# A full 128-row tile for the low part of the keys in a split-precision attention

## The chip, the cores and the metric

The program runs on one NeuronCore of one Trainium2 chip. Its time is device microseconds (us) from the first to the last of its work, as the median of three runs. One more execution was recorded by the hardware profiler; all rows below come from that one. TensorE (PE in the rows; PEld is its loading of stationary operands) multiplies, VectorE (DVE) and ScalarE (ACT) do the elementwise work, GpSimd (POOL) does a part of it, and SyncE (SP) issues the transfers.

## The reference, cut to what matters

One layer of a diffusion backbone on 1024 latent tokens (a grid of 16 rows by 64 columns) and 128 context tokens, width 1024, 8 heads of 64. Queries and keys come from one projection; a latent query attends in one softmax to a window of keys around it and to 128 cached context keys; a context query attends to the 128 context tokens:

```python
s_band = jnp.einsum('bhqd,bhikd->bhqik', q_r, k_b).astype(jnp.float32) * SCALE
s_band = s_band + bias[None].astype(jnp.float32)
s_band = jnp.where(col_mask[None, None, :, None, :], s_band, -jnp.inf)
s_ctx = jnp.einsum('bhqd,bhld->bhql', q_r, k_ctx).astype(jnp.float32) * SCALE
s = jnp.concatenate([s_band.reshape(b, h, GRID_W, n_band), s_ctx], axis=-1)
p = jax.nn.softmax(s, axis=-1).astype(v.dtype)
```

Beside the attention there are a gated short convolution, projections of both, two normalisations and a feed-forward part of width 4096. All of it is float32.

## The kernel before, in words

**Split precision.** A float32 operand is held as two parts: a high part rounded to float32r (a cast) and a low part (the value minus the high part). A product is the sum of high by high, high by low and low by high, each a TensorE matmul into the same accumulator.

**Stages.** First the modulation and the values V (to some 85 us of the span). Then the queries and keys of head 0 as dense products (lines 364, 366 and 368, the three matmuls of a contraction block). Then the attention proper: 8 heads of 9 units each, 72 units. Units 0 to 7 of a head are (column block, row half): 128 latent queries against 384 window keys and the 128 cached keys. Unit 8 holds the 128 context queries against 128 context keys. After the attention come gates and projections, the output projection, and the feed-forward part.

**One unit.** `scores(n)` issues the matmuls of the scores; VectorE adds bias and mask and takes the row extremum (line 561), ScalarE takes the exponential (563), VectorE the reciprocal and the scaling (566, 567). One unit later `transposes(n)` turns the probabilities by TensorE (576), and ScalarE and VectorE split them (210, 211). Two units later, for each pair of units, `pv` multiplies them with the values (600 to 610, and 593 and 594 for the context). Between these, TensorE gets dense matmuls: 72 for each head, the projection of the next head's queries and keys, dealt out by the table SHARES; for the last head it is a gate product. All orders are written out by hand; each engine runs its own list in that order, and waits by semaphores.

**The operands of a score.** A head has 64 dimensions, half of the 128 rows of TensorE's array. Tile `qs` holds the high part of the queries on 64 rows and their low part on the other 64; which half is which depends on the parity of the head (`ev` is the half of the high part). Tile `kh` holds the high part of the keys twice, on both halves, so that one matmul over 128 rows gives high by high and low by high together (lines 554, 555, and 549 for the context). Tile `kl` holds the low part of the keys on the rows `ev` alone, and a head of the other parity uses the other half of the same tile. Its matmuls (556, 557, and 550 for the context) therefore take 64 rows of `qs` and 64 rows of `kl`. The four matmuls of a unit are 384, 128, 384 and 128 columns wide and go to one bank. `kl` is written by VectorE (line 439, out of a dense product) and GpSimd (line 436, the cached keys).

Of the kernel before, what the change touches and what calls it, by code (L numbers as in the profile page):

```python
# [12 lines left out]
F32 = mybir.dt.float32  # L13
F32R = mybir.dt.float32r
# [4 lines left out]
P = 128  # L19
D = 1024  # L20
KB = D // P
NLAT = 1024
NCTX = 128
# [14 lines left out]

WCOL = (0, 8, 24, 32)
MOFF = (16, 8, 8, 0)  # L40
# Dense products issued with each unit of a head's attention, which spread them evenly over its length.
SHARES = (8, 8, 9, 7, 9, 7, 9, 7, 8)
CTYPE = (0, 1, 1, 2)
# Per chunk of tokens: (row half, first row in the half, offset in the chunk, rows; no rows: the context).
QPIECES = (((0, 0, 0, 6),), ((0, 6, 0, 2), (1, 0, 128, 4)), ((1, 4, 0, 4), (0, 0, 256, 0)))


def tail_len(c):
    """Blocks of the second feed-forward product that a chunk of tokens ends with, token tile by token tile."""
    return 5 if c == NCH - 1 else 2  # L50


def window_masks():
    """Additive masks of the clamped window: [row half a][column kind][query (8 x 16)][key (12 x 32)]."""
    out = np.zeros((2, 3, P, 12 * 32), np.float32)
    for a in range(2):
        for kind, c in enumerate((0, 1, 3)):
            for r in range(8):
                qr = 8 * a + r
                sr = min(max(qr - WR // 2, 0), ROWS - WR)  # L60
                kr = 4 * a + np.arange(12)
                okr = (kr >= sr) & (kr < sr + WR)
                for q in range(16):
                    qc = 16 * c + q
                    sc = min(max(qc - WC // 2, 0), GW - WC)
                    kc = WCOL[c] + np.arange(32)
                    okc = (kc >= sc) & (kc < sc + WC)
                    out[a, kind, r * 16 + q] = np.where(okr[:, None] & okc[None, :], 0.0, NEG).reshape(-1)
    return out


class Ring:
    """Weight blocks [128, <=1024]: loaded in the order of their use, split into two float32r parts."""

    def __init__(self, nc, pool, name, seq, raw_bufs, bufs):
        self.nc, self.pool, self.name, self.seq = nc, pool, name, seq
# [4 lines left out]
        self.more = None  # L81

    def extend(self, pool):
        """From here on one more buffer of each kind, in a pool of its own."""
        self.more = pool, self.nload, self.nhi

    def tile(self, dtype, tag, i, bufs, kind):
# [61 lines left out]
def emit(nc, tc, ctx, aps, outs):  # L149
# [60 lines left out]
        nc.scalar.copy(hi, src)  # L210
        vec.tensor_tensor(out=lo, in0=src, in1=f32(hi), op=ALU.subtract)  # L211

    # ---------------------------------------------------------------- constants
    ident = const.tile([P, P], F32, name="ident")
    ones = const.tile([P, 2], F32, name="ones")
    vec.memset(ones, 1.0)
# [14 lines left out]

    h = [act_chunk() for _ in range(NCH)]

    # ---------------------------------------------------------------- modulation of the mixers' input, V
    with ExitStack() as s0:
        p0 = pool_on(s0, "p0", side="right")
        act(sil, cs, AF.Sigmoid)
# [116 lines left out]
                v_mm(b, t, kb, kb == 0, kb == KB - 1)  # L354
            v_out(b, t)

    # ---------------------------------------------------------------- dense products, channel-major
    def chunk_mm(b, w, c, kbs=KB, woff=0, src=None, first=True, last=True):
        hi, lo = w
        a = src or h[c]  # L360
# [11 lines left out]
        for _ in g:  # L372
            pass

    # ---------------------------------------------------------------- attention
    with ExitStack() as s2:
        p2 = pool_on(s2, "p2", side="right")
        mask = p2.tile([P, 6, 384], BF16, name="mask")
        kl = p2.tile([P, NTOK + NCTX], F32R, name="kl")
        bms = [p2.tile([P, 512], F32, name=f"bm{i}") for i in range(2)]  # L380
        for b_ in bms:
            pl.memset(b_, 0.0)
# [8 lines left out]
        jobs = []  # L391

        def flush_act():
            """Issue ScalarE's parts of the waiting small jobs; returns VectorE's."""
            todo, jobs[:] = jobs[:], []
            for fa_, _ in todo:
                fa_()
            return [fd for _, fd in todo]
# [5 lines left out]
        def dense_qk(hh):  # L404
            ck = cks.pop(hh)
            w = ring.take(ahead=0)
            qs = p2.tile([P, NTOK], F32R, tag="qs", name=f"qs{hh}", bufs=2)
            kh = p2.tile([P, NTOK + NCTX], F32R, tag="kh", name=f"kh{hh}", bufs=2)
            ev = slice(0, 64) if hh % 2 == 0 else slice(64, 128)
            od = slice(64, 128) if hh % 2 == 0 else slice(0, 64)  # L410
            qk[hh] = (qs, kh, ev)
            def pieces(c, b):
                for a, r0, o, nr in QPIECES[c]:
                    if nr:
                        src = b[0:64, o:o + nr * GW].rearrange("p (r c q) -> p r c q", c=4, q=16)
                        yield (src,) + tuple(x[:, :NLAT].rearrange("p (a c r q) -> p a r c q", a=2, c=4, r=8)
                                             [:, a, r0:r0 + nr] for x in (qs[ev], qs[od], f32(qs)[ev]))
                    else:
                        yield b[0:64, o:o + NCTX], qs[ev, NLAT:], qs[od, NLAT:], f32(qs)[ev, NLAT:]

            def qk_act(c, b):
                sl = slice(c * CH, (c + 1) * CH)
                if c == 1:
                    nc.scalar.copy(kh[:, NTOK:], ck)
                nc.scalar.copy(kh[64:128, sl], b[64:128, :CH])
                for src, dh, _, _ in pieces(c, b):
                    nc.scalar.copy(dh, src)
                if c == NCH - 1:
                    kf = p2.tile([P, NCTX], F32, tag="kf", name=f"kf{hh}", bufs=1)
                    nc.scalar.copy(kf[64:128], b[64:128, CH - NCTX:CH])  # L430
                    dma(outs["nk"][hh], kf[64:128])

            def qk_vec(c, b):
                sl = slice(c * CH, (c + 1) * CH)
                if c == 1:
                    pl.tensor_tensor(out=kl[ev, NTOK:], in0=ck[ev], in1=f32(kh)[ev, NTOK:], op=ALU.subtract)
                for src, _, dl, dhf in pieces(c, b):
                    vec.tensor_tensor(out=dl, in0=src, in1=dhf, op=ALU.subtract)
                vec.tensor_tensor(out=kl[ev, sl], in0=b[64:128, :CH], in1=f32(kh)[64:128, sl], op=ALU.subtract)
                (pl if hh else vec).tensor_copy(kh[0:64, sl], f32(kh)[64:128, sl])  # L440

            for c in range(NCH):
                b = next_dense()
                yield from chunk_mm(b, w, c)
                jobs.append((lambda c=c, b=b: qk_act(c, b), lambda c=c, b=b: qk_vec(c, b)))
# [93 lines left out]

        def scores(n):  # L540
            hh, c, a = units[n]
            qs, kh, ev = qk[hh]
            sb = bank(3 + n % 2)
            s = p2.tile([P, 512], F32, tag="s", name=f"s{n}", bufs=2)
            st = p2.tile([P, 4], F32, tag="st", name=f"st{n}", bufs=4)
            qa = q_ap(qs, c, a)
            qh = q_ap(qs[ev], c, a)
            if c == 4:
                mm(sb[:, :P], lhsT=qa, rhs=kh[:, NLAT:NTOK], start=True, stop=False)
                mm(sb[:, :P], lhsT=qh, rhs=kl[ev, NLAT:NTOK], start=False, stop=True)  # L550
                w = P
                bm = bms[0][:, 384:512]
            else:
                mm(sb[:, :384], lhsT=qa, rhs=k_ap(kh, c, a), start=True, stop=False)
                mm(sb[:, 384:], lhsT=qa, rhs=kh[:, NTOK:], start=False, stop=False)
                mm(sb[:, :384], lhsT=qh, rhs=k_ap(kl[ev], c, a), start=False, stop=False)  # L556
                mm(sb[:, 384:], lhsT=qh, rhs=kl[ev, NTOK:], start=False, stop=True)
                w = 512
                bm = bms[n % 2]
            dve = flush_act()  # L560
# [129 lines left out]
        run(filler)  # L690
        flush_all()

    # ---------------------------------------------------------------- mixers' projections
    mB = pool_on(ctx, "mB", bufs=4)
    acp = pool_on(s3, "acp", side="right", bufs=8)
    tp = pool_on(s3, "tp", side="right", bufs=2)
# [15 lines left out]
                later.popleft()()  # L712

    def gemv_rest():
        """The modulation after the mixers: g1, sh2, sc2, g2 of both conditionings, 512 columns at a time."""
        ones_r = gp.tile([P, 2], F32R, name="ones_r")
        nc.scalar.copy(ones_r, ones)
        for g in range(8):
# [200 lines left out]
            split(mc[0][:, j], mc[1][:, j], mix[j][:, csl(c)])  # L919
    s3.close()  # L920

    # ---------------------------------------------------------------- output projection, first norm
    x9 = pool_on(ctx, "x9")
    wx = pool_on(ctx, "wx")
    ring.extend(wx)
# [19 lines left out]
    HALVES = (slice(0, 512), slice(512, 1024))  # L945

    def norm(t, gr, br, out, done=None, adder=vec, parts=(slice(0, D),)):
        """Closures that normalise t (in place) and write t * g + b to out."""
        m = tmp(fp, [P, 4], "bag", 6)

        def stats():
# [21 lines left out]
        return [stats, scale, apply, last]  # L973

    def weave(lists):
        """The closures of three tiles in an order in which no engine waits long for another."""
        a, b, c = lists
        return [a[0], a[1], b[0], a[2], b[1], c[0], b[2], c[1], a[3], c[2], b[3], lambda: None, c[3]]

# [36 lines left out]
        return go  # L1016

    def token_mm(banks, a, i, w, first, last, kb=None):
        """banks[half] += a[token tile i]^T @ w, a = (hi, lo) parts [128, (kb,) tokens]."""
        ts_ = slice(i * P, (i + 1) * P)  # L1020
        ah, al = (a[0][:, kb, ts_], a[1][:, kb, ts_]) if kb is not None else (a[0][:, ts_], a[1][:, ts_])
        for half in range(2):
# [27 lines left out]
        bg.extend(weave(parts))  # L1050
        later.extend(make_h2(c, kb) for kb in range(KB))

    # ---------------------------------------------------------------- feed-forward, second norm
    s6 = ExitStack()
    rows2 = {}

# [6 lines left out]
        rows2["ln2b"] = row(r2, "ln2b", aps["ln2b"])  # L1063

    def residual(t):
        """x1 becomes ALPHA * x1 + b2 * g2, all of the second sum but the product."""
        def go():
            if t == 8:
                r = tmp(fp, [P, D], "lnt", 3)
# [39 lines left out]
        return [first] + q[1:]  # L1109

    def ln2_final(t, ps):
        """The last token tile: each half of its columns as soon as its products are done."""
        r = tmp(fp, [P, D], "lnt", 3)
        m = tmp(fp, [P, 4], "bag", 6)
        s_ = tmp(fp, [P, 2, 6], "bst", 2)
# [148 lines left out]
```

## Time and profile before

| what | value |
|---|---|
| median of three runs | 1708.21 us (1706.99 to 1708.92) |
| span of the profiled execution | 1707.4 us |
| TensorE busy with matmuls | 1674.1 us, 98% of the span |
| VectorE, ScalarE, GpSimd busy | 965.0, 666.8, 219.2 us |
| heaviest lines | 364, 366, 368: 1632 matmuls each, some 552 us each |
| mean traffic to and from memory | 115 GB/s |

The page gives the span of the profiled execution and no other time of it. The median of the runs is 0.8 us above that span, and this is what lies around it. A busy share is an average over the stages; the rows below come mostly from the attention, between 97 and 328 us.

### The profile page before, as it was taken

To read this page: it belongs to the slowest core of one execution; us is meant where nothing else is said; L and a number is where in the kernel's file an instruction comes from. 1 tells how busy PE (TensorE), PEld (TensorE's weight loads), DVE (VectorE), ACT (ScalarE), POOL (GpSimd) and SP (SyncE) were. 2 spreads that over 40 slices of the span, in tenths; PEclk is the share of its full clock that TensorE was granted. 3 is DMA by queue.
4 is the path that set the end of the run, shared out by engine and by line. 5 is a ranking of instruction groups with operands and counts; after the bars stand their busy time and mean duration, and the time that the engine had idled before them with its cause. 6 is when DMAs were issued, how large, how long until landed. Compare 5 with 4: busy or idle time off the path is not lost.

```text
span 1707.4 us, 23233 instructions
## 1 busy us (share of the span) xinstructions
PE 1674.1 (98%) x8984; PEld 1534.1 (90%) x8984; DVE 965.0 (57%) x1504; ACT 666.8 (39%) x1132; POOL 219.2 (13%) x218
## 2 busy tenths in 40 slices
PE   7999999999999999999999999999999999999997
PEld 5799999999999999998779999998999998999996
DVE  6567778654555565245786556546644445644446
ACT  5366767611122121133454453333433333433332
POOL 2145555200000002110220000000100000100002
PEclk9999999999999999999999999999999999999998
DMA  8332121123222222116433345333443333444332
GB/s 315 132 90 68 46 68 47 45 95 104 83 91 81 87 81 93 51 38 225 145 123 124 123 138 171 130 131 110 166 142 124 124 123 124 136 163 131 126 123 74
DMA packets 86327, 196.01 MB, mean 115 GB/s; under 512 B 32305, under 2 KB 33969, under 8 KB 86217
## 3 DMA queue, kind: packets, MB, share of 16 engines
q1 hardware_dynamic: 86072, 194.52, 34.4%
q8 instruction: 70, 1.15, 0.3%
q14 instruction: 41, 0.33, 0.1%
q10 hardware_dynamic: 144, 0.01, 0.0%
HBM read 186.86 MB, written 7.63 MB: 114 GB/s over the span
## 4 chain that ended last, share of the span: by engine, by line
PE 92%; DVE 5%; DMA 1%; ACT 1%; issue 1%; ACTq 0%; DVEq 0%; SPq 0%
PE ps L368 17%; PE ps L364 17%; PE ps L366 17%; PE ps L1024 8%; PE ps L1023 8%; PE ps L1026 8%; PE ps L800 2%; PE ps L801 2%; PE ps L802 2%; PE ps L576 2%; PE ps L556 1%; DVE wl L126 1%; PE ps L301 1%; DMA wr<-wo 1%; PE ps L303 1%; PE ps L260 1%
## 5 line engine op out<-in xcount | busy, mean ns | idle before, releaser
L364 PE MATMUL ps<-ahi,wh 128*128 128x384 f32 x1632 | 552.1, 338 | 0.0
L368 PE MATMUL ps<-ahi,wl 128*128 128x384 f32 x1632 | 551.9, 338 | 0.0
L366 PE MATMUL ps<-alo,wh 128*128 128x384 f32 x1632 | 551.2, 338 | 0.0
L126 DVE TENSOR_TENSOR wl<-wr,wh 128x1024 fp32r<-128x1024 f32 (+1 forms) x258 | 321.6, 1271 | 120.3 <-ACT wh L113 120.1
L364 PEld LDWEIGHTS ps<-ahi,wh 128*128 128x128 f32 x1632 | 306.5, 188 | 8.6 <-issue 1.4
L366 PEld LDWEIGHTS ps<-alo,wh 128*128 128x128 f32 x1632 | 306.5, 188 | 7.1
L368 PEld LDWEIGHTS ps<-ahi,wl 128*128 128x128 f32 x1632 | 306.4, 188 | 3.2
L113 ACT CAST wh<-wr 128x1024 fp32r<-128x1024 f32 (+1 forms) x266 | 262.6, 1022 | 41.4 <-DMA wr<-wo 18.4
L1023 PE MATMUL ps<-wh,fh 128*128 128x512 f32 x550 | 215.3, 391 | 1.3 <-ACT fh L210 1.3
L1024 PE MATMUL ps<-wl,fh 128*128 128x512 f32 x550 | 216.1, 393 | 0.0
L1086 ACT ACTIVATE rt<-ps,b1c 128x384 f32<-128x384 f32 x96 | 55.9, 582 | 402.5 <-PE ps L368 402.5
L1087 DVE TENSOR_TENSOR rt<-rt 128x384 f32<-128x384 f32 x96 | 53.6, 558 | 273.0 <-ACT rt L1086 273.0
L1026 PE MATMUL ps<-wh,fl 128*128 128x512 f32 x550 | 170.5, 391 | 0.0
L1026 PEld LDWEIGHTS ps<-wh,fl 128*128 128x128 f32 x550 | 103.3, 188 | 21.9
L1023 PEld LDWEIGHTS ps<-wh,fh 128*128 128x128 f32 x550 | 103.2, 188 | 21.7 <-ACT fh L210 2.1
L1024 PEld LDWEIGHTS ps<-wl,fh 128*128 128x128 f32 x550 | 103.3, 188 | 18.9
L965 POOL TENSOR_TENSOR lnt<-lnt,ln2g 128x1024 f32<-128x1024 f32 x8 | 19.2, 2397 | 718.7 <-ACT lnt L964 704.5
L741 DVE SCALAR_TENSOR_TENSOR acc<-wmb,sil,acc 128x512 f32<-128x512 f32 x112 | 81.6, 773 | 27.5 <-DMA wmb<-wmb 27.5
L211 DVE TENSOR_TENSOR fl<-rt,fh 128x384 fp32r<-128x384 f32 x92 | 51.4, 559 | 53.3 <-ACT fh L210 53.3
L210 ACT CAST fh<-rt 128x384 fp32r<-128x384 f32 x92 | 47.2, 513 | 57.9 <-DVE rt L1087 57.9
L563 ACT ACTIVATE s<-s,st 128x512 f32<-128x512 f32 (+1 forms) x72 | 49.6, 688 | 51.3 <-DVE st L561 51.3
L800 PE MATMUL ps<-ach,wh 128*128 128x384 f32 x192 | 65.1, 339 | 0.0
(217 smaller groups left out, 2094.4 us busy)
## 6 DMA issues: line engine op xcount, KB each, us to landing
wr<-w SPq DMA_DIRECT2D x192, 512.0 KB
wmb<-wmb SPq DMA_DIRECT2D x64, 256.0 KB
wr<-wo SPq DMA_DIRECT2D x24, 512.0 KB
mr<-wma SPq DMA_DIRECT2D x16, 512.0 KB
xt<-xt SPq DMA_DIRECT2D x8, 576.0 KB
xk<-xk SPq DMA_DIRECT2D x9, 512.0 KB
vraw<-vd SPq DMA_DIRECT2D x136, 32.0 KB
wr<-wqk SPq DMA_DIRECT2D x8, 512.0 KB
```

Source lines behind the costliest of these rows:

```text
L113: self.nc.scalar.copy(hi[:, :w], self.raw[i][:, :w])
L126: engine.tensor_tensor(out=lo[:, :w], in0=self.raw.pop(i)[:, :w], in1=hi.bitcast(F32)[:, :w], op=ALU.subtract)
L364: mm(b[:, :CH], lhsT=hi[:, ws], rhs=a[0][:, kb, :], start=first and kb == 0, stop=False)
L366: mm(b[:, :CH], lhsT=hi[:, ws], rhs=a[1][:, kb, :], start=False, stop=False)
L368: mm(b[:, :CH], lhsT=lo[:, ws], rhs=a[0][:, kb, :], start=False, stop=last and kb == n - 1)
L741: vec.scalar_tensor_tensor(out=a, in0=t, scalar=sil[:, k, cond:cond + 1], in1=a, op0=ALU.mult, op1=ALU.add)
L800: mm(b[:, :CH], lhsT=hi[:, ws], rhs=parts[kb][0][:, cs_], start=kb == 0, stop=False)
L1023: mm(banks[half], lhsT=ah, rhs=w[0][:, HALVES[half]], start=first, stop=False)
L1024: mm(banks[half], lhsT=ah, rhs=w[1][:, HALVES[half]], start=False, stop=False)
L1026: mm(banks[half], lhsT=al, rhs=w[0][:, HALVES[half]], start=False, stop=last)
L1086: act(rt, b[:, :CH], AF.Relu, bias=b1c[:, f:f + 1])
L1087: vec.tensor_tensor(out=rt, in0=rt, in1=rt, op=ALU.mult)
```

## The change

The one tile `kl` becomes two, `kls[0]` and `kls[1]`, one for each parity of the head. The half that a parity does not use is set to zero once by GpSimd before the attention. The matmuls on the low part of the keys take all 128 rows of `qs` and of the tile; the low part of the queries then meets zeros. The writers of `kl` write the same rows as before, in the tile of their head. The second tile takes 5120 more bytes of each partition, which moves the tiles that are allocated behind it. Comments were removed too, and the lines behind this place have numbers higher by three or four.

```diff
-        kl = p2.tile([P, NTOK + NCTX], F32R, name="kl")
+        kls = [p2.tile([P, NTOK + NCTX], F32R, name=f"kl{i}") for i in range(2)]
+        for i in range(2):
+            pl.memset(kls[i][64 - 64 * i:128 - 64 * i].bitcast(F32), 0.0)
...
-            qk[hh] = (qs, kh, ev)
+            kl = kls[hh % 2]
+            qk[hh] = (qs, kh, kl)
...
             qa = q_ap(qs, c, a)
-            qh = q_ap(qs[ev], c, a)
             if c == 4:
                 mm(sb[:, :P], lhsT=qa, rhs=kh[:, NLAT:NTOK], start=True, stop=False)
-                mm(sb[:, :P], lhsT=qh, rhs=kl[ev, NLAT:NTOK], start=False, stop=True)
+                mm(sb[:, :P], lhsT=qa, rhs=kl[:, NLAT:NTOK], start=False, stop=True)
...
-                mm(sb[:, :384], lhsT=qh, rhs=k_ap(kl[ev], c, a), start=False, stop=False)
-                mm(sb[:, 384:], lhsT=qh, rhs=kl[ev, NTOK:], start=False, stop=True)
+                mm(sb[:, :384], lhsT=qa, rhs=k_ap(kl, c, a), start=False, stop=False)
+                mm(sb[:, 384:], lhsT=qa, rhs=kl[:, NTOK:], start=False, stop=True)
```

On GpSimd, at the head of the attention, this stands in its list before (bm are the bias tiles, kl the low keys, kh the high keys, ck the cached keys, E the bias table; what an instruction waits for is in brackets):

```order
L382 MEMSET bm_790 128x512 [waits PE_49]
L382 MEMSET bm_791 128x512 [waits DMAHW2_49,DMAHW1_49,DVE_49]
L529 TENSOR_TENSOR bm_790<-E_801,mask 128x384 [waits DMAHW1_49,Activation_49,Pool_49]
L436 TENSOR_TENSOR kl<-ck_799,kh_824 64x128 [waits DMAHW7_49,PE_49,Activation_49]
L529 TENSOR_TENSOR bm_791<-E_801,mask 128x384 [waits Pool_49]
```

and this after the change:

```order
L382 MEMSET kl_789 64x1280 [waits Pool_49]
L382 MEMSET kl_790 64x1280 [waits PE_49]
L385 MEMSET bm_793 128x512 [waits Pool_49]
L385 MEMSET bm_794 128x512 [waits DMAHW2_49,DMAHW1_49,DVE_49]
L533 TENSOR_TENSOR bm_793<-E_804,mask 128x384 [waits DMAHW1_49,Activation_49,Pool_49]
L440 TENSOR_TENSOR kl_789<-ck_802,kh_827 64x128 [waits DMAHW7_49,Activation_49]
L533 TENSOR_TENSOR bm_794<-E_804,mask 128x384 [waits Pool_49]
```

Two instructions are added ahead of the others; the wait for PE that the first bias tile had stands at the second of them. On TensorE the order is the same instruction for instruction. At the first unit of the first head it reads before (qs the queries, ps the accumulator):

```order
L554 MATMUL ps_932<-kh_824,qs_823 128x384 [waits DVE_49,Activation_49]
L555 MATMUL ps_932<-kh_824,qs_823 128x128
L556 MATMUL ps_932<-kl,qs_823 128x384
L557 MATMUL ps_932<-kl,qs_823 128x128 [waits Pool_49]
L364 MATMUL ps_961<-ahi_94,wh_857 128x384 [waits PE_49]
```

and after the change:

```order
L557 MATMUL ps_935<-kh_827,qs_826 128x384 [waits DVE_49,Activation_49]
L558 MATMUL ps_935<-kh_827,qs_826 128x128
L559 MATMUL ps_935<-kl_789,qs_826 128x384 [waits Pool_49]
L560 MATMUL ps_935<-kl_789,qs_826 128x128 [waits Pool_49]
L364 MATMUL ps_964<-ahi_94,wh_860 128x384 [waits PE_49]
```

The third matmul has got a wait for GpSimd, once in the program. On VectorE, ScalarE and SyncE the lists and what their instructions wait for read the same.

## Rows read from the trace of the kernel before

**Rows 1.** Windows: busy us (x instructions) per engine; then clock, DMA share, GB/s

```profile
97.50:328.00 230.50, 228.94 (x1449) 207.11 (x1447) 179.42 (x459) 158.11 (x395) 118.91 (x146) 1.00 0.20 54
375.00:450.00 75.00, 75.00 (x429) 74.12 (x429) 37.70 (x58) 13.38 (x23) 0.00 (x0) 1.00 0.27 92
```

**Rows 2.** Waits of TensorE, 97.5 to 328: total us, times, longest

```profile
PE ps L554 <- DVE kh L440: 0.8, 1, 0.8
PE ps L593 <- DVE attnT L621: 0.8, 1, 0.8
```

**Rows 3.** Timeline of TensorE's matmuls around one unit: start, duration, engine, line, tiles, shapes

```profile
125.63 0.34 PE L554 MATMUL ps<-kh,qs 128*128 128x384 f32 x1
125.81 0.22 PE L555 MATMUL ps<-kh,qs 128*128 128x128 f32 x1
125.96 0.44 PE L556 MATMUL ps<-kl,qs 64*128 64x384 f32 x1
126.24 0.22 PE L557 MATMUL ps<-kl,qs 64*128 64x128 f32 x1
126.39 0.45 PE L364 MATMUL ps<-ahi,wh 128*128 128x384 f32 x1
126.67 0.34 PE L366 MATMUL ps<-alo,wh 128*128 128x384 f32 x1
```

**Rows 4.** Timeline of TensorE's weight loads around the same unit

```profile
125.63 0.19 PEld L555 LDWEIGHTS ps<-kh,qs 128*128 128x128 f32 x1
125.96 0.18 PEld L556 LDWEIGHTS ps<-kl,qs 64*128 64x128 f32 x1
...
126.39 0.19 PEld L364 LDWEIGHTS ps<-ahi,wh 128*128 128x128 f32 x1
```

**Rows 5.** Groups by shape, TensorE, 97.5 to 325: busy us, mean ns | idle

```profile
L556 PE MATMUL ps<-kl,qs 64*128 64x384 f32 x64 | 28.3, 442 | 0.0
```

**Rows 6.** Timeline of TensorE in the modulation: a matmul over 4 rows

```profile
54.82 0.60 PE L268 MATMUL ps<-sel,rows 4*128 4x2 f32 x4
55.35 0.50 PE L301 MATMUL ps<-wh,ahi 128*128 128x512 f32 x1
55.69 0.39 PE L302 MATMUL ps<-wl,ahi 128*128 128x512 f32 x1
```

**Rows 7.** Timeline of TensorE: one 128-column transpose between dense matmuls

```profile
127.03 0.35 PE L364 MATMUL ps<-ahi,wh 128*128 128x384 f32 x1
127.21 0.27 PE L576 MATMUL ps<-ident,s 128*128 128x128 f32 x1
...
127.49 0.33 PE L368 MATMUL ps<-ahi,wl 128*128 128x384 f32 x1
```

**Rows 8.** Timeline of TensorE: a context unit

```profile
123.22 0.28 PE L549 MATMUL ps<-kh,qs 128*128 128x128 f32 x1
123.42 0.32 PE L550 MATMUL ps<-kl,qs 64*128 64x128 f32 x1
...
123.96 0.34 PE L368 MATMUL ps<-ahi,wl 128*128 128x384 f32 x1
```

**Rows 9.** Timeline of VectorE in the seventh and eighth unit of a head

```profile
205.25 1.08 DVE L567 TENSOR_SCALAR s<-s,st 128x512 f32<-128x512 f32 x1
...
206.85 0.68 DVE L561 CUSTOM_DVE_ANT_0 s<-ps,bm 128x512 f32<-128x512 f32 x1
...
208.98 0.49 DVE L567 TENSOR_SCALAR s<-s,st 128x512 f32<-128x512 f32 x1
```

**Rows 10.** Timeline of TensorE: the transposes of these two units

```profile
206.96 0.60 PE L576 MATMUL ps<-ident,s 128*128 128x128 f32 x4
...
210.28 0.60 PE L576 MATMUL ps<-ident,s 128*128 128x128 f32 x4
```

**Rows 11.** Timeline of GpSimd at the head of the attention

```profile
80.90 0.99 POOL L382 MEMSET bm<- 128x512 f32 x2 [24.82 <-PE ps L302]
94.00 0.92 POOL L529 TENSOR_TENSOR bm<-E,mask 128x384 f32<-128x384 f32 x1 [12.11 <-DMA vraw<-vd]
```

More of the change, by code (lines that the diff above doesn't have):

```diff
@@ L541, in scores @@
             hh, c, a = units[n]
-            qs, kh, ev = qk[hh]
+            qs, kh, kl = qk[hh]
             sb = bank(3 + n % 2)
```

## The prediction

> **What bounds the kernel now.** I first cut the span into stages by busy time, since the change touches only the attention. From 97.5 to 328 us TensorE is busy 228.94 of 230.50 us, VectorE 179.42, ScalarE 158.11 and GpSimd 118.91 [rows 1]: TensorE is the limit, the next engine has a fifth of the stage free, and TensorE's granted clock is 1.00, its 2.4 GHz level, throughout. Busy time alone doesn't prove it, because a matmul that waits for its weights counts as busy; so I read the waits next. In the whole stage TensorE waits for others only twice, 0.8 us each [rows 2]. A microsecond taken from TensorE's own list in this stage therefore comes off the end, as long as the others keep up. What a matmul should cost is read in a stretch of dense matmuls, nearly all of 384 columns: 429 in 75.00 us, so 0.175 us each [rows 1], whose weights are all there in time.
>
> Then I read the timeline of one unit by starts, not by durations (durations overlap) [rows 3]. L554 to L555 takes 0.18, as it should. L555, 128 columns, to L556 takes 0.15. L556, 384 columns, to L557 takes 0.28 in place of 0.175. L557 to the dense L364 takes 0.15, and L364 to L366 again 0.28. The loads say why: the load for L555 starts with the matmul before it (125.63, the start of L554), but the load for L556 starts only at 125.96, with its own matmul, and so does that for L364 at 126.39 [rows 4, 3]. These are the two places where a 128-row operand is followed by a 64-row one or the other way about. It is so in every unit: L556 has a mean of 442 ns over all 64 [rows 5], against 0.34 us for L554 of the same width [rows 3]. It isn't the bank or the strided keys: the dense L364 behind the unit, another bank and plain operands, lasts 0.45 us as well [rows 3], and in the modulation a matmul over 4 rows is followed by a 512-column one of 0.50 us, where the next has 0.39 [rows 6].
>
> **The change part by part.** *The score matmuls.* All four take 128 rows, so both places go. What the same four matmuls then cost has to be taken from full-row neighbours. A 384-column one is 0.175. A 128-column one between wider ones is shown by the single transpose: from the dense matmul ahead of it to the second behind it 127.49 - 127.03 = 0.46 us, less two of 0.175, is 0.11 [rows 7]; it doesn't reach 0.175/3 = 0.058, since the next load takes longer than 128 columns. The zeros stream like any other rows: L554, full, and L556, half, differ only by the exposed load. From the start of L555 to the second dense matmul before: 126.67 - 125.81 = 0.86 [rows 3]. After: 0.11 + 0.175 + 0.11 + 0.175 = 0.57. That is 0.29 us for each of 64 units, 18.6 us.
>
> *The context units.* From L549 to the second dense matmul 123.96 - 123.22 = 0.74 [rows 8]. After: 0.11 + 0.11 + 0.175, and 0.06 by which the record of L549 (0.28, against 0.22 for L555) stands ahead of its weights: 0.455. That is 0.285 for each of 8, 2.3 us. Together 20.9 us.
>
> The ends of this term: below, nothing, if the row count isn't the cause; above, a 128-column matmul at its bare 0.058, another 0.104 in each unit, 28 us in all. I take 0.11, which full-row rows of this stage show; the transpose differs from a score matmul only in its operand.
>
> *What could take it back.* Between the end of the scores and the transposes of the same unit lie the leaving of this unit's 64-row tile (0.15 + 0.28 against 0.11 + 0.175, so 0.145) and the next unit's four matmuls (0.29): VectorE and ScalarE lose some 0.43 us of time to finish. The tightest place that repeats is the seventh unit of a head, where VectorE's L567 takes 1.08 us: it ends at 206.33 and its transposes start at 206.96 [rows 9, 10], so 0.63 are free now and 0.2 will be. In the eighth unit VectorE is already late (its L561 at 206.85 starts as soon as it is done with the unit before): L567 ends at 209.47, the transposes start at 210.28 [rows 9, 10], 0.81 free, from which 0.43 goes and another 0.29 because VectorE doesn't move while TensorE does: about 0.1 is left. So the cover just holds. The first of the two waits of rows 2, in the second unit of all, gets longer, since its releaser runs in VectorE's pace; 0.1 to 0.3 us. I put 0.4 us on all of this.
>
> *The added memsets.* Two of 64x1280 on GpSimd. Two of 128x512 took 0.99 us [rows 11]; by columns two of 1280 take 2.5, at the least (by elements) 1.2. GpSimd sits idle for 12.11 us before its first bias tile at 94.00 [rows 11], so they cost nothing; without that cover 2.5 us once. The new wait of the first L556 for GpSimd comes at 98, long after. The queues of SyncE, VectorE and ScalarE stay as they are, and so does every stage behind the attention, which starts earlier and is otherwise the same.
>
> Sum: 20.9 - 0.4 = 20.5 us off a span of 1707.4, so 1686.9; with the 0.8 us that the median stands above it, 1687.7 us.
>
> **A rule that speaks against it.** In the rows, loads are hidden within one row count: in the dense stretches each load starts with the matmul before it (the full-row load for L555 at 125.63 under the full-row L554) [rows 3, 4]. The Trainium skill ("TensorE: Matmul & The Clock Gate", "The mechanism" in Part 3) says the reverse, that a weight load overlaps a running matmul only when the two use different row groups. By it the full-row loads of L556, L557 and L364 would all be exposed. The trace contradicts it, by 429 matmuls at 0.175 us.
>
> **The rivals.** *The loads of four matmuls on one set of rows stay exposed.* Then the two costs stay, and L557, hidden now by its 64-row neighbour, pays the 0.105 of an exposed load too (0.28 - 0.175): 72 times 0.105 is 7.6 us more, 1715.8. It decides if the load for the third score matmul starts with its own matmul. Against it stand the dense rows; for it only that no row shows one stationary operand loaded four times in a row (twice, for L554 and L555, it is hidden). It is the case by the rule above. Chance 0.03.
>
> *VectorE takes the place of the limit.* If its lateness adds up from the seventh unit to the first of the next head, and the margins of 0.1 and 0.2 us are overdrawn, TensorE waits at some four units of each head by up to 0.3 us each: 8 x 4 x 0.3 = 9.6 back, 1697. For it: 179 us of work in a stage that shrinks to 210 us. Against it: VectorE waits again for TensorE in the other units, so it catches up once a head. Chance 0.08.
>
> *Nothing comes of it.* The cost would lie in something else at these two places, or in the half-width tile being only one of two triggers: 1708, or half of the gain, 1698. Rows 6 speak against it. Chance 0.03 for the first.
>
> **How the numbers follow.** 0.86 for the forecast with its own spread: 0.02 us each way in the price of a unit (starts are rounded to 0.01, five of them) is 1.5 us, the give-back may be 0 to 3. That is 1685 to 1691. The 128-column price below 0.11 would bring it to 1684, part of the second rival to 1694. The range is 1684 to 1694. A measurement of this kernel can tell about 0.2%, 3.4 us; all cases but the first and third rivals are faster by more: 0.94 faster, 0.03 the same, 0.03 slower.
>
> **What would show it.** In the profile after, the third score matmul has 128 rows, a load that starts with the second, and a mean of about 0.34 us in place of 0.442; the dense matmul behind the fourth has 0.34 to 0.42. A head takes some 2.6 us less. TensorE's waits in the stage stay under 2 us; if waits for L567's tile s turn up at the seventh and eighth unit of a head by tenths of a microsecond, the second rival is at work. The forecast is wrong if the loads still start with their own matmuls, or if the time of the stages behind moves by over 1 us.

## The result and the profile after

The change makes the kernel faster, by less than forecast: 1694.97 us (median of four runs, 1693.59 to 1695.93) against 1708.49 for the kernel before in the same comparison. The ratio is 0.9922, 95% interval 0.9908 to 0.9936. That is 13.5 us where 20.5 were forecast, and 1 us outside the range. The profiled execution has a span of 1694.1 us, 13.3 less than before.

The unit first. The score matmuls of the kernel after are lines 557 to 560 (552 and 553 for the context). TensorE's timeline where the scores of a head's eighth unit are followed by the transposes of its seventh:

```profile
171.55 0.22 PE L558 MATMUL ps<-kh,qs 128*128 128x128 f32 x1
171.61 0.39 PE L559 MATMUL ps<-kl,qs 128*128 128x384 f32 x1
171.84 0.22 PE L560 MATMUL ps<-kl,qs 128*128 128x128 f32 x1
171.89 0.39 PE L364 MATMUL ps<-ahi,wh 128*128 128x384 f32 x1
172.12 0.34 PE L366 MATMUL ps<-alo,wh 128*128 128x384 f32 x1
...
172.49 0.34 PE L364 MATMUL ps<-ahi,wh 128*128 128x384 f32 x1
173.41 0.63 PE L579 MATMUL ps<-ident,s 128*128 128x128 f32 x4 [0.58 <-DVE s L570]
```

and the weight loads of the same stretch:

```profile
171.55 0.19 PEld L559 LDWEIGHTS ps<-kl,qs 128*128 128x128 f32 x1
...
171.84 0.19 PEld L364 LDWEIGHTS ps<-ahi,wh 128*128 128x128 f32 x1
```

The load for the third score matmul starts with the second (171.55), that for the dense matmul with the fourth (171.84); before, each started with its own [rows 4]. From the second score matmul to the second dense one it is 172.12 - 171.55 = 0.57 us, where it was 0.86 [rows 3]. But behind the unit something new stands: after the dense matmul at 172.49 the transposes should start 0.175 later; they start 0.92 later, and wait for VectorE.

The stage as a whole, by the window of the attention (columns as in [rows 1]), and TensorE's waits from 97 to 320 us:

```profile
97.30:314.05 216.75, 210.42 (x1447) 203.50 (x1447) 175.60 (x459) 157.96 (x395) 118.59 (x146) 1.00 0.22 58
```

```profile
PE ps L579 <- DVE s L570: 4.4, 8, 0.7
PE ps L557 <- DVE kh L444: 1.1, 1, 1.1
PE ps L596 <- DVE attnT L624: 0.8, 1, 0.8
```

Two waits have become ten [rows 2]: once a head the transposes wait for the scaled probabilities. (By the starts it is about 0.72 us at the transposes of the seventh unit and another 0.08 at those of the eighth.) The waits of VectorE show the other side. First before, from 112 to 300 us (total, times, longest), then after:

```profile
DVE st L566 <- ACT s L563: 21.4, 37, 0.9
DVE s L561 <- PE ps L557: 5.9, 12, 0.6
DVE ptl L211 <- ACT pth L210: 3.7, 7, 0.5
```

```profile
DVE st L569 <- ACT s L566: 24.0, 41, 0.9
DVE ptl L211 <- ACT pth L210: 3.6, 7, 0.5
```

The middle line is gone: VectorE no longer waits for the scores at all. And the chain of waits from 118 to 280 us, as shares by line, is TensorE from end to end before:

```profile
by line: PE ps L366 17.2%; PE ps L364 17.1%; PE ps L368 16.8%; PE ps L576 12.7%; PE ps L556 10.3%; PE ps L610 7.1%; PE ps L554 5.6%; PE ps L600 3.2%; PE ps L606 2.3%; PE ps L608 2.3%; PE ps L557 1.7%; PE ps L555 1.6%; PE ps L550 0.9%; PE ps
```

and after it runs mostly through VectorE's extremum (564) and scaling (570), ScalarE's exponential (566) and the short latencies between engines ("issue"):

```profile
by line: issue 15.1%; DVE s L564 13.6%; DVE s L570 12.9%; ACT s L566 10.9%; PE ps L579 5.3%; PE ps L366 4.4%; PE ps L368 3.9%; ACT pth L210 3.6%; PE ps L364 3.5%; DVE st L569 3.5%; DVE qs L442 3.2%; DVE kl L443 3.1%; PE ps L613 2.9%; ACT E
```

A head is what to count in, from here on as the mean of four heads, by the starts of the first score matmuls of the third and the seventh head. Before:

```profile
154.24 0.34 PE L554 MATMUL ps<-kh,qs 128*128 128x384 f32 x1
...
268.60 0.34 PE L554 MATMUL ps<-kh,qs 128*128 128x384 f32 x1
```

(268.60 - 154.24) / 4 = 28.59 us. After:

```profile
150.90 0.34 PE L557 MATMUL ps<-kh,qs 128*128 128x384 f32 x1
...
258.19 0.34 PE L557 MATMUL ps<-kh,qs 128*128 128x384 f32 x1
```

(258.19 - 150.90) / 4 = 26.82 us. TensorE's own list should be 28.59 less the measured price of nine units, 0.285 each for eight and 0.286 for the context unit (means over 64 and 8 units), so 26.02. So 0.80 us of each head is missing, 6.4 us in all.

What VectorE does at that place in the next head (the brackets give its idle time before an instruction and what ended it):

```profile
196.40 0.69 DVE L211 TENSOR_TENSOR ptl<-ps,pth 128x512 fp32r<-128x512 f32 x1 [0.52 <-ACT pth L210]
197.01 0.68 DVE L564 CUSTOM_DVE_ANT_0 s<-ps,bm 128x512 f32<-128x512 f32 x1
...
197.73 0.42 DVE L624 TENSOR_TENSOR attnT<-ps,otmp 64x256 f32<-64x256 f32 x1
198.58 0.17 DVE L569 RECIPROCAL st<-st 128x1 f32<-128x1 f32 x1 [0.43 <-ACT s L566]
198.78 1.30 DVE L570 TENSOR_SCALAR s<-s,st 128x512 f32<-128x512 f32 x1
200.00 0.68 DVE L211 TENSOR_TENSOR ptl<-ps,pth 128x512 fp32r<-128x512 f32 x1
```

and GpSimd beside it:

```profile
197.41 2.39 POOL L126 TENSOR_TENSOR wl<-wr,wh 128x1024 fp32r<-128x1024 f32 x1
```

The scaling (570) takes 0.49 us elsewhere. Here it ends at 200.08, 0.28 after GpSimd's subtraction of the next head's weights (199.80). Before, the scaling took 1.08 us and ended at 206.33 [rows 9], also 0.28 behind GpSimd; only nobody waited for it (its transposes start at 206.96 [rows 10]):

```profile
203.65 2.40 POOL L126 TENSOR_TENSOR wl<-wr,wh 128x1024 fp32r<-128x1024 f32 x1
```

### The profile page after: what moved, and what is told of

It reads as the page before. It is cut to its first block, busy times and chain, and to the rows that moved or that the text cites. A ratio compares the mean times of both kernels' runs of the same rounds, so it can differ in the third digit from the quotient of the medians.

```text
span 1694.1 us, 23235 instructions
## 1 busy us (share of the span) xinstructions
PE 1656.6 (98%) x8984; PEld 1532.0 (90%) x8984; DVE 961.0 (57%) x1504; ACT 666.5 (39%) x1132; POOL 221.1 (13%) x220
## 4 chain that ended last, share of the span: by engine, by line
PE 81%; DVE 10%; ACT 3%; issue 3%; DMA 2%; SPq 0%; POOL 0%; ACTq 0%; POOLq 0%; DVEq 0%
PE ps L368 15%; PE ps L366 15%; PE ps L364 15%; PE ps L1027 8%; PE ps L1029 8%; PE ps L1026 8%; PE ps L803 2%; PE ps L805 2%; PE ps L804 2%; DVE s L564 2%; DVE s L570 1%; ACT s L566 1%; DVE wl L126 1%; DMA wr<-wo 1%; PE ps L301 1%
```

## The experiments

Two theories stood against each other after the first look. *Local*: only this one collision of scaling and subtraction in the seventh unit costs, TensorE is else the limit. *Loop*: VectorE and ScalarE work through a chain that goes on from unit to unit (extremum, exponential, cast of the last unit's transposed probabilities, subtraction, next extremum; 2.8 to 2.9 us in a unit without other work, where TensorE now needs 2.66 and needed 2.95 before), which over a head is as long as 26.8 us, the collision included. The 2.8 us are read from VectorE's extrema in the kernel after, from the second to the fourth unit of a head:

```profile
181.98 0.68 DVE L564 CUSTOM_DVE_ANT_0 s<-ps,bm 128x512 f32<-128x512 f32 x1
...
184.78 0.68 DVE L564 CUSTOM_DVE_ANT_0 s<-ps,bm 128x512 f32<-128x512 f32 x1
...
187.57 0.68 DVE L564 CUSTOM_DVE_ANT_0 s<-ps,bm 128x512 f32<-128x512 f32 x1
```

Ratios are against the kernel before, with their 95% intervals; a head is counted in each run's trace as above.

**e2, the tiles alone.** The kernel after with `lhsT=qh` and `kl[ev]` (64 rows) put back in all low-part matmuls; the two tiles and the memsets stay.

Expected: 

> Two tiles and two memsets, but the low-part matmuls take 64 rows as in the kernel before. If the time came from the two changes of row count in each unit (0.14 us each), they are back: 1708.5, the third score matmul at 442 ns again. Rival, that the moved tiles or the separate tiles for the two parities of the head did it: nearer 1695.

Measured: 1707.95 us, ratio 0.9999 (0.9991 to 1.0008); a head 28.59. Tiles and memsets cost and give nothing; all of the gain is in the row count.

**e1, one of the two matmuls.**

```diff
-                mm(sb[:, 384:], lhsT=qa, rhs=kl[:, NTOK:], start=False, stop=True)
+                mm(sb[:, 384:], lhsT=qh, rhs=kl[ev, NTOK:], start=False, stop=True)
```

Expected: 

> Third score matmul over 128 rows, only the fourth (128 columns) over 64; context units full. Theory that each change of row count costs about 0.14 us, however many 64-row matmuls stand between: two changes per unit as before, 64 units at the old price, the 8 context units keep 2.3 us: 1706. Rival, that each 64-row matmul pays for its own weight load: half of the 18 us stays, 1697.

Measured: 1707.96 us, ratio 0.9997 (0.9988 to 1.0006); a head 28.62. TensorE in one unit (here 560 to 562 are the second to the fourth score matmul):

```profile
185.31 0.22 PE L560 MATMUL ps<-kh,qs 128*128 128x128 f32 x1
185.37 0.39 PE L561 MATMUL ps<-kl,qs 128*128 128x384 f32 x1
185.69 0.32 PE L562 MATMUL ps<-kl,qs 64*128 64x128 f32 x1
185.95 0.45 PE L368 MATMUL ps<-ahi,wl 128*128 128x384 f32 x1
186.23 0.34 PE L364 MATMUL ps<-ahi,wh 128*128 128x384 f32 x1
```

From the second score matmul to the second dense one 0.92 us, no better than the 0.86 of before: one narrow matmul of 64 rows makes as many changes of row count as two, and brings back all of the cost. It is the change that is paid for, not the matmul. The run is not faster than the kernel before as 1706 would have been, though its context units are cheap: each of the other units takes some 0.04 us longer than before (2.99 in place of 2.95 for a short one), which eats up their 2.3 us. Why is open.

**e4, GpSimd's subtraction in four pieces** of 256 columns (`split_lo` loops over column slices).

Expected: 

> The kernel after, with GpSimd's subtraction of 128x1024 in the attention cut into four of 256 columns. Collision theory (the scaling on VectorE in the seventh unit takes 1.30 in place of 0.49 us because it can't run beside that subtraction, and this stall of 0.72 us on TensorE per head is all that was given back): the scaling takes 0.5 to 1.1, the stall goes, 8 x 0.72 = 5.8 us, 1689. Loop theory (VectorE's in-order chain with ScalarE's exponential is longer than TensorE's list over the whole head, 26.8 against 26.1 us): the chain gets up to 0.8 us per head shorter, also about 1689. If TensorE's own list were longer than I read: 1695.

Measured: 1692.41 us, ratio 0.9906 (0.9893 to 0.9920). The scaling still takes 1.05 us (0.56 too long in place of 0.81), a head 26.57. The head got shorter by just what the stretch lost, 0.25. Half of what both theories had expected, since a scaling still waits for a piece.

**e3, no scaling in the third unit.**

```diff
-            vec.tensor_scalar(out=s[:, :w], in0=s[:, :w], scalar1=st[:, 2:3], scalar2=None, op0=ALU.mult)
+            if n % 9 != 2:
+                vec.tensor_scalar(out=s[:, :w], in0=s[:, :w], scalar1=st[:, 2:3], scalar2=None, op0=ALU.mult)
```

Expected: 

> The kernel after without the scaling of the probabilities in the third unit of each head (these stay unnormalised): 0.49 us less on VectorE, four units ahead of the stall. Loop theory: the chain of VectorE and ScalarE is shorter by up to 0.49 us per head, 8 x 0.49 = 3.9 us, 1691, and the stall of the seventh unit's transposes falls from 0.7 to some 0.2 us. Collision theory: the stall is made in the seventh unit alone, 1695.

Measured: 1694.30 us, ratio 0.9915 (0.9902 to 0.9929), a head 26.82 as in the kernel after. That looks like the local theory, but VectorE's waits say why nothing came of it:

```profile
DVE st L569 <- ACT s L566: 23.3, 40, 0.9
DVE ptl L211 <- ACT pth L210: 6.7, 14, 0.5
```

Seven more waits of half a microsecond for ScalarE's cast have come: the subtraction stands behind both the scaling and the cast, and these two end at the same time. With the scaling gone the cast holds it. The 1691 of the loop theory was missed, and the reason was found afterwards. The run took out a branch of the loop that had an equal beside it, so it doesn't decide.

**e5, work moved in front of the stalled transposes.**

```diff
-            adv(share - share // 2)
+            late = share if n % 9 == 7 else share - share // 2
+            adv(late)
```

Expected: 

> The kernel after, but in the eighth unit of each head the three dense matmuls behind the transposes stand ahead of them; nothing else moves. Local theory (only the stall of 0.72 us at these transposes is lost, TensorE's list would else be the limit): 3 x 0.175 us of it are filled with work, 8 x 0.52 = 4.2 us, 1691. Loop theory (the chain exponential on ScalarE, cast of the transposed probabilities, subtraction on VectorE, next extremum is as long as a head, 26.8 us, whatever TensorE does): 1695.

Measured: 1693.93 us, ratio 0.9917 (0.9902 to 0.9932); a head 26.84. The work was put where the stall is, and the seventh unit's transposes wait some 0.2 us in place of 0.7. But now those of the eighth unit start 0.74 us behind their dense matmul, where it was 0.26 in the kernel after:

```profile
174.73 0.33 PE L366 MATMUL ps<-alo,wh 128*128 128x384 f32 x1
175.47 0.63 PE L579 MATMUL ps<-ident,s 128*128 128x128 f32 x4 [0.41 <-DVE s L570]
```

The wait moved on by one unit and the head didn't get shorter: the local theory, that TensorE's list is the limit but for one stall, falls. That a longer chain than these two units is at work has to come from the next runs.

**e6, VectorE's subtraction in the gap**, one unit later, between extremum and reciprocal.

```diff
-            split(ph[:, sl], pl_[:, sl], tb[:, :ng * P])
+            nc.scalar.copy(ph[:, sl], tb[:, :ng * P])
+            low = lambda: vec.tensor_tensor(out=pl_[:, sl], in0=tb[:, :ng * P], in1=f32(ph[:, sl]), op=ALU.subtract)
+            if n + 2 < len(units):
+                jobs.insert(0, (lambda: None, low))
+            else:
+                low()
```

Expected: 

> The kernel after with VectorE's subtraction of the probabilities' low part (line 211, 0.69 us) issued one unit later, between the extremum and the reciprocal, where VectorE waits 0.4 to 0.9 us for ScalarE's exponential. Loop theory: the next extremum no longer waits for cast and subtraction, the chain falls under TensorE's list, a head takes 26.0 us: 8 x 0.78 = 6.2 us, 1689, and VectorE waits for TensorE again. Local theory: the scaling still ends with GpSimd's subtraction, whose start ScalarE's list sets: 1694 to 1695. If the values' matmuls then wait for the later low part, less than either.

Measured: 1691.96 us, ratio 0.9906 (0.9889 to 0.9922); a head 26.44, half of what the loop theory expected. VectorE waits for TensorE's scores again, its extrema start 0.15 us behind the scores in the first seven units as in the kernel before, and the chain of waits from 118 to 280 us is TensorE's once more:

```profile
DVE s L564 <- PE ps L560: 11.2, 33, 1.1
DVE s L564 <- POOL cv L515: 7.5, 7, 1.1
DVE st L569 <- ACT s L566: 5.1, 16, 0.4
```

```profile
by line: PE ps L368 16.6%; PE ps L364 16.5%; PE ps L366 16.4%; PE ps L579 14.4%; PE ps L618 8.1%; PE ps L559 6.8%; PE ps L557 6.0%; PE ps L608 4.5%; PE ps L616 2.6%; PE ps L614 2.6%; PE ps L560 1.8%; PE ps L558 1.8%; PE ps L553 0.5%; PE ps
```

What is left of the other half can be read too. The collision itself stays, and the transposes of the seventh unit still stand 0.42 us behind their dense matmul in place of 0.175:

```profile
196.32 1.17 DVE L570 TENSOR_SCALAR s<-s,st 128x512 f32<-128x512 f32 x1
...
197.21 0.34 PE L364 MATMUL ps<-ahi,wh 128*128 128x384 f32 x1
197.63 0.63 PE L579 MATMUL ps<-ident,s 128*128 128x128 f32 x4
```

That is 0.24 us. Another 0.2 are the values' matmuls, which wait for the later low part, the case that the expectation names last; the next run shows them. Together this is about the 0.42 by which a head is above TensorE's 26.02.

**e7, gap and pieces together.**

Expected: 

> The subtraction in the gap and GpSimd's subtraction in four pieces together. Loop theory: nothing more to gain beyond TensorE's list: 1689, the same as the gap alone within 1 us. Local theory: the gain of the pieces alone, 1692.

Measured: 1689.63 us, ratio 0.9893 (0.9879 to 0.9908); a head 26.24; TensorE has no wait for the scaling left. It is the fastest version, 5.3 us (0.3%) below the kernel after by the medians, though the two intervals touch. (TensorE's granted clock is 0.95 in the attention of this trace, near its 2.4 GHz level, and 1.00 in the kernel after. From 420 to 500 us, at 0.95 and 1.00 too, matmuls start 0.175 us apart in both, so the heads are compared as they stand.) The last 0.2 us of a head above TensorE's 26.02 are the values' matmuls over the low part:

```profile
197.91 0.68 DVE L590 TENSOR_TENSOR ptl<-ps,pth 128x512 fp32r<-128x512 f32 x1
...
198.54 0.27 PE L612 MATMUL ps<-pth,cv 128*128 128x256 f32 x1
198.65 0.38 PE L612 MATMUL ps<-ptl,cv 128*128 128x256 f32 x1
198.87 0.22 PE L618 MATMUL ps<-pth,vw 128*128 128x128 f32 x1
```

The subtraction that was moved ends at 198.59, 0.06 us before the first matmul that reads it (0.65 and more in the kernel after), and the next matmul stands 0.22 behind that one in place of 0.12. It is so in two of the four groups of a head, 0.2 us; in one of the four heads a group comes another 0.19 late.

**e9, the same gap in the kernel before.**

Expected: 

> The kernel before with the subtraction of the probabilities' low part moved into VectorE's gap, as in the run on the kernel after that gained by it. If the chain of VectorE and ScalarE became the limit only through the change (26.8 us a head against TensorE's 28.6 before), a shorter chain gives nothing here: 1708, within 1 us, a head stays at 28.6 us. If the gap saves time by itself (less contention on the accumulators, say), about 3 us less as there: 1705.

Measured: 1708.72 us, ratio 1.0001 (0.9991 to 1.0010); a head 28.61. Where TensorE's list is the longer one, the shorter chain is worth nothing. This run and e6 together show that the limit moved.

**e8, the split three units earlier** (`split_hi` at k == 1, `split_lo` at k == 3).

Expected: 

> The kernel after with the split of the next head's weights three units earlier: ScalarE's cast in the second unit, GpSimd's subtraction in the fourth, where the transposes have 0.94 us to spare in place of 0.15. Local theory: the stretched scaling is absorbed there, the stall goes: 5.8 us, 1689. Loop theory: the chain of VectorE and ScalarE is as long as before, the stall turns up in another unit: 1693 to 1695.

Measured: 1707.03 us, ratio 0.9993 (0.9983 to 1.0002): slower than either theory said, nearly all of the gain lost. VectorE, the two stretched scalings of a head:

```profile
189.60 1.02 DVE L570 TENSOR_SCALAR s<-s,st 128x512 f32<-128x512 f32 x1
...
193.21 2.30 DVE L570 TENSOR_SCALAR s<-s,st 128x512 f32<-128x512 f32 x1
```

0.53 + 1.81 = 2.34 us of stretch, and a head of 28.44; 26.01 + 2.34 would be 28.35. They stand in the third and fourth unit, where scaling and transposes were 0.47 and 0.95 us apart in the kernel after, of which 0.15 always pass. Had this spare time taken up what it could, 0.32 + 0.80, a head would be some 27.2 us (an estimate: 26.02 + 2.34 - 1.12). It didn't. The chain of waits of this run also passes through a weight transfer, so the size isn't clean; that made the next run worth having.

**e10, only GpSimd's subtraction one unit earlier** (`split_lo` at k == 5).

Expected: 

> The kernel after with GpSimd's subtraction of the next head's weights one unit earlier and nothing else moved (ScalarE's cast stays). It then meets the scaling of the sixth unit, in which the transposes had 2.1 us to spare before and 1.2 after. Chain theory: a head takes 26.0 us plus all that scalings are stretched in it, wherever they stand (so far 26.82 with 0.81, 26.57 with 0.55): with a stretch of some 1.5 us 27.5 us a head, 8 x 0.7 us slower than the kernel after, 1700. Local theory: the spare time of the sixth unit takes it up, 1689 to 1692.

Measured: 1700.57 us, ratio 0.9955 (0.9938 to 0.9971), where the loop theory had 1700; a head 27.41. The scaling takes 2.47 us (1.98 too long) and again ends 0.28 behind the subtraction:

```profile
197.37 2.47 DVE L570 TENSOR_SCALAR s<-s,st 128x512 f32<-128x512 f32 x1
```

```profile
197.18 2.38 POOL L126 TENSOR_TENSOR wl<-wr,wh 128x1024 fp32r<-128x1024 f32 x1
```

It isn't the full 1.98 that a head pays over 26.01, but 1.40: in this unit VectorE waited 0.52 us for ScalarE's cast anyway (the first line of VectorE's rows above), and this wait is gone from the run's list. So the hit on 1700 is in part luck: it was forecast with a stretch of 1.5, and the full 1.98 would have made 28.0 us a head. The local theory doesn't fit either: of the 1.20 us in the sixth unit 1.05 could be taken up, which leaves 26.95 us (26.02 + 1.98 - 1.05, an estimate).

**e11, eight pieces.**

Expected: 

> The kernel after with GpSimd's subtraction in eight pieces of 128 columns in place of one. If the scaling waits only for the piece that runs, the stretch falls from 0.55 (four pieces) to some 0.3 us and a head to 26.3 us by the chain theory: 1690.5. If the scaling waits for all pieces that are queued, it is as with one piece or worse: 1695. By the local theory the stall falls by as much as the stretch, so 1690 to 1691 too: this run sizes the stretch, it doesn't tell the two apart.

Measured: 1692.23 us, ratio 0.9908 (0.9893 to 0.9923), as with four pieces; a head 26.63. Heads of 26.16 and 27.10 us alternate. The seventh unit's scaling is stretched by only 0.14 us in each; but in every other head the eighth unit's (0.69) and the one of the context unit before it (0.47) now run beside GpSimd's later additions. That is 0.72 us a head, 26.73 by the sum, so the gain of the smaller pieces was lost to other collisions, and the run sizes the stretch only loosely.

## Why the prediction was wrong

**The price of a unit was right.** Forecast 0.57 us from the second score matmul to the second dense one, measured 0.57; over all units 0.285 us gained for 0.29, in the context units 0.286 for 0.285. 72 units give 20.5 us for 20.9. The parts of the sum fell otherwise: behind a 128-column score matmul the next starts after 0.06 us and behind a 384-column one after 0.23, where 0.11 and 0.175 were forecast; each pair has 0.29. So the third score matmul lasts 0.395 us on the mean, not the 0.34 that was named as a sign. That a change of row count exposes a load was right, and e1 and e2 show it apart from all else. The Trainium skill ("TensorEngine Tiling (Array Packing)", "Key Properties") says that a change of the tiling mode drains the array. No row here names the mode; if a 64-row matmul among full ones is such a change, the 0.14 us for each change and e1, where the number of changes counts, agree with it. The rule against the change from the prediction, that of the Trainium skill ("TensorE: Matmul & The Clock Gate", "The mechanism" in Part 3) that loads are hidden only across row groups, is contradicted by the loads of the kernel after, too: they start with the matmul before them, at 171.55 and 171.84.

**"What could take it back" is the step that failed.** It gave 0.4 us; it was 6.7 (8 x 0.80, and 0.3 at the first wait of rows 2, which grew from 0.8 to 1.1 us as said). That leaves 13.8 of 20.5 us; 13.5 were measured, and in the two traces the attention, from the first score matmul to the last of the values' matmuls, went from 230.8 to 217.2 us. Three things were wrong in it. I took VectorE to be on time in all units but the seventh and eighth, and asked there what was left. That was read off a kernel in which TensorE needed 2.95 us for its short units, a little more than the chain of VectorE and ScalarE takes; with 2.66 the chain is late in every unit (the mean start of the extremum behind the end of the scores went from 0.15 to between 0.33 and 0.71 us in the first six), and the lateness was already there when the seventh began (0.69 us). Second, 1.08 us for the seventh scaling was taken for a duration. Most of it is a wait: the scaling ends 0.28 us behind GpSimd's subtraction, and on GpSimd's list that stands behind line 502, which waits for a cast of ScalarE (0.22 us in the kernel after), not for TensorE. So it ate 0.81 us where I had 0.59. Third, 0.63 us to spare counted in some 0.15 us that pass between the end of a scaling and its transposes even when these wait (the smallest distance after the change). The three close the sum for the seventh unit: 0.63 us, less 0.15, the 0.43 of the forecast, 0.69 - 0.15 = 0.54 of lateness and 0.81 - 0.59 = 0.22 of stretch, is 0.71 short, and its transposes wait about 0.72.

**The rival with a chance of 0.08 is what happened.** VectorE takes the place of the limit, and lateness adds up. It went by the busy share (179 of 210 us) and so got too small a chance: the chain is long not by work but by its order, in which VectorE and ScalarE wait for each other (24.0 us from 112 to 300 us for the exponential alone). Its sign came true (waits for the tile s at the seventh and eighth unit). Its size, 9.6 us given back at four units of a head, was too large; it was 6.7, nearly all at one unit. What holds for it over the runs: a head takes 26.01 us plus the stretch of the scalings in it, for the kernel after (0.81), e3 (0.82), e4 (0.56) and e5 (0.83) to 0.01 us. With other stretches it holds less well: e8 (2.34) is 0.09 above it, e11 (0.72) 0.10 below, and e10 (1.98) 0.58 below, most of it the 0.52 of a wait that was there before. That the chain without any stretch would be as long as TensorE's 26.02 is chance, and since a stretch remains, pieces alone can't give back everything.

**Memsets, tiles, stages behind.** As forecast, nothing. For the first two e2 shows it; from the end of the attention to the end of the span it is 1379.7 us after and 1379.1 before.

## What to carry to other kernels

A matmul over fewer rows than its neighbours costs at both ends, here 0.14 us each on a list whose steps are 0.06 to 0.23 us: filling the rows with zeros is cheaper, but one narrow matmul left in brings all of it back. Before counting a saving on the engine that is the limit, add up the longest cycle through the other engines in their own order, latencies included, over a whole period; VectorE's busy share of 80% didn't show it here. An instruction whose duration varies, as this scaling's, may be waiting for something: find what it ends with, and count that as an edge of the chain.

## What the runs showed of the hardware that I had not expected

VectorE's scaling from memory to memory (128x512, 0.49 us) doesn't finish while GpSimd subtracts: it took 1.08, 1.30 and 2.47 us, and ended 0.28 us behind GpSimd each time. GpSimd's addition of the bias (line 533) does the same: 1.02 us in e8, and 0.28 behind. Others aren't touched: line 624, which reads one operand from the accumulators, takes its 0.42 us beside the same subtraction. The Trainium skill ("SBUF — State Buffer", "Who interferes with whom") says that VectorE in its two-port mode and GpSimd lock each other out for a whole instruction, and that VectorE with at most one operand from SBUF outside that mode doesn't contend; these rows agree, though none names the mode, and 0.28 us is less than the 0.49 of a whole scaling. Cutting GpSimd's instruction in four helped from 0.81 to 0.56 us; in eight, the seventh unit's stretch fell to 0.14, but other scalings of the head were stretched.
